# Seven block products in place of eight in 15 of the feed-forward pairs of a two-layer diffusion trunk

## The chip, the cores and the metric

The kernel runs on one core of a Trainium2 chip. The metric is the device time of one execution in microseconds (us). Engines are named as the profile names them: PE is TensorE's matrix multiplies, PEld its weight loads, DVE is VectorE, ACT is ScalarE, POOL is GpSimd, SP is SyncE, which issues the large loads.

## What is computed

Two layers over 256 latent tokens (stream 0) and 256 context tokens (stream 1), model width 1024. Each layer is a gated feed-forward sub-layer (FFN), a mixer of attention and retention, and a second FFN. The last FFN runs for the latent tokens alone. So three FFNs (layer 0 first and second, layer 1 first) have both streams, and one has a single stream.

```
def swiglu_sublayer(h, shift, scale, gate, g_pre, g_post, wi, wo):
    u = rmsnorm(h, g_pre) * (1 + scale) + shift
    a, b = jnp.split(u @ wi, 2, axis=-1)
    y = (jax.nn.silu(a) * b) @ wo
    return h + FFN_RESIDUAL * gate * rmsnorm(y, g_post)
```

The hidden width of an FFN is 22 x 128. `shift`, `scale` and `gate` come from `silu(c) @ ada_w[l] + ada_b[l]`, nine vectors for each layer, which must be ready when the sub-layer that uses them starts.

## The kernel before

**Precision.** Every float32 operand of a large matrix product is split in two float32r parts, hi (a copy, ACT) and lo = x - hi (a subtraction, DVE). A product is then three matmuls: hi hi, hi lo, lo hi.

**An FFN.** The normalized input u lies transposed in SBUF as two tiles, `uh` and `ul`, each 128 partitions x 2 streams x 8 k-tiles x 256 tokens. In the up stage a loop over f = 2 to 21 calls `pair(f)` (line 729; pairs 0 and 1 go through `first` or `first_of_all`). A pair loads two weight tiles of 128 x 1024 (512 KB each; line 160), splits each (`load_w`: hi on ACT, line 167, lo on DVE, line 168), and multiplies: for each of the two tiles and each of the 8 k-tiles `uT` (line 200) issues three matmuls over all 512 tokens, 48 matmuls for the pair. Then `gated` (line 479) forms silu(a) * b on ACT (line 480) and DVE (line 481) into a tile `g`, which is kept until the down stage. In the last FFN only 256 tokens are there, and the same 48 matmuls have 256 columns. There `uu` lies 48 elements further on in its tiles (`SHIFT`, lines 93 and 486).

The down stage (line 866 on) computes y in two halves of 512 columns. Each half takes 11 chunks of two f: `prep` loads and splits one 128 x 1024 tile of `wo` and splits two `g` tiles (lines 879 and 880), and four token tiles take six matmuls each (lines 889 to 891). The last three chunks of a half are done token tile by token tile.

**Work that fills DVE.** The products of `ada_w` with the conditioning are done on DVE in steps (`ada_steps`, line 314): a step loads 512 KB and runs two SCALAR_TENSOR_TENSOR of 128 x 1024 (line 324), one for each stream. `ada.step(n)` puts n steps into the program at a place. `fill` gives their number for the up and the down stage of an FFN: (34, 14) for the first FFN of layer 0, (32, 8) for the second, (30, 10) for the first of layer 1. In the up stage they are spread over the pairs (line 864), in the down stage over the first 12 of 16 chunks: the first eight of half 0 and the first four of half 1 (line 905).

**Order and buffers.** The program is written once, in order; a scheduler at compile time gives each engine its own fixed order, an earlier place in the program first among what it takes to be ready, so work can move ahead of its place where its buffers are free. Buffers are rings: 7 raw tiles for all large loads, 3 `whi` and 3 `wlo`, 2 each of `t4k0` and `t4k1`, 26 tiles of 2 KB (`t2k`: the 22 `g` tiles and short-lived ones), 8 banks of PSUM, and a tile `gm` that serves gates, attention outputs and raw weights in turn.

Of the kernel before, what the change touches and what calls it, by code (L numbers as in the profile page):

```python
# [8 lines left out]
F32 = mybir.dt.float32  # L9
R = mybir.dt.float32r  # L10
# [3 lines left out]
AX = mybir.AxisListType  # L14

P = 128
L = 2
D = 1024
KT = 8
# [13 lines left out]
def hybrid_kernel(ctx: ExitStack, tc: tile.TileContext, A: dict, out: bass.AP):  # L33
# [123 lines left out]
    def load_raw(src, shape):  # L157
        raw = wp.tile([P, 1024], F32, tag="raw", name="raw", bufs=7)
        n = shape[0] * shape[1]
        loads.append(nc.sync.dma_start(raw[:, :n], src).ins)  # L160
        return raw[:, :n].rearrange("p (a b) -> p a b", a=shape[0])

    def load_w(src, shape):
        raw = load_raw(src, shape)
# [240 lines left out]
    def pre_norm(sub, s):  # L405
# [3 lines left out]
            last = pre_norm_part(sub, s, xn, k2)  # L409
        return last  # L410

    def pre_norm_part(sub, s, xn, k2):
        pt = psum([P, 2, 256], "ps_tr")
        for k in (0, 1):
            q, c0 = divmod(128 * (k2 + k), 512)
            for i in (0, 1):
                last = nc.tensor.transpose(pt[:, k, 128 * i:128 * i + 128], xn[i][q][:, c0:c0 + 128], ident)
        uf = t2k([P, 2, 256], name="uf")
        for k in (0, 1):
            sc, sh = scT[:, sub, s, k2 + k:k2 + k + 1], shT[:, sub, s, k2 + k:k2 + k + 1]  # L420
            nc.scalar.activation(uf[:, k, :], pt[:, k, :], AF.Identity, scale=sc, bias=sh)
        hi = uu[0][:, s, k2:k2 + 2, :]
        nc.vector.tensor_copy(hi, uf)
        behind[0] = nc.vector.tensor_sub(uu[1][:, s, k2:k2 + 2, :], uf, hi.bitcast(F32)).ins
        return last.ins

    def post_half(y, gates, t, half, part):


        junk = small([P, 512], "junk", 1)  # L430
        ss = small([P, 1], "ssy", 12)
        nc.scalar.activation(junk, y, AF.Square, scale=D ** -0.5, accum_out=ss)
        if half:
            st = small([P, 1], "ssum", 12)
            nc.vector.scalar_tensor_tensor(out=st, in0=part[0][0], scalar=RMS_EPS, in1=ss, op0=ALU.add, op1=ALU.add)
            ss = rsqrt(st)
        x = t2k([P, 512], name="x")
        nc.vector.tensor_mul(x, y, gates[t // 2][:, 512 * half:512 * half + 512])
        part[half] = ss, x
# [43 lines left out]
    def last_head(then, l, mm, ys, gates, parts):  # L483
# [28 lines left out]
        ssy = {}  # L512

        def square(t, half):
            junk = small([P, 512], "junk", 1)
            ssy[t, half] = small([P, 1], "ssy", 12)
            nc.scalar.activation(junk, ys[half, t], AF.Square, scale=D ** -0.5, accum_out=ssy[t, half])

# [185 lines left out]
    def ffn(l, name, sub, streams, fill, nxt):  # L704
# [6 lines left out]
        def first():  # L711
# [14 lines left out]
                    gated(gf[f][:, cs], *ps)  # L726
            g.extend(gf)

        def pair(f):
            w = [next_w.pop()] if next_w else [load(f, 0)]  # L730
            w.append(load(f, 1))
            ps = [psum([P, n], "ps_up") for _ in range(2)]
            for ab in range(2):
                for k in range(KT):
                    uT(ps[ab], w[ab], k, 0, streams)
            g.append(t2k([P, n], name="g"))
            gated(g[f], *ps)

        def first_of_all():
# [17 lines left out]
            def modulated(j):  # L757


                ks, pt = slice(2 * j, 2 * j + 2), pts.pop(j)  # L760
                uf = [t2k([P, 2, 256], name="uf") for _ in range(2)]
                for outs in [(uh[:, 0, ks, :], uh[:, 1, ks, :]), (uf[1], uf[0])]:
                    if outs[0] is uf[1]:
                        yield
                    for k in (0, 1):
                        kk = 2 * j + k
                        sc, sh = ([x[:, 0, s, kk:kk + 1] for s in range(2)] for x in (scT, shT))
                        a, v = (0, 1) if outs[0] is not uf[1] else (1, 0)
                        nc.scalar.activation(outs[0][:, k, :], pt[a][:, k, :], AF.Identity, scale=sc[a], bias=sh[a])
                        nc.vector.tensor_scalar(out=outs[1][:, k, :], in0=pt[v][:, k, :], scalar1=sc[v],  # L770
                                                scalar2=sh[v], op0=ALU.mult, op1=ALU.add)
                yield
                for s in range(2):
                    behind[0] = nc.vector.tensor_sub(ul[:, s, ks, :], uf[s], uh[:, s, ks, :].bitcast(F32)).ins

            def mm_hi(j, *ws):
# [79 lines left out]
        for f in range(2, NFF):  # L856
# [3 lines left out]
                with tc.issue_after(behind[0]):  # L860
                    constants(loads[-1])
            f0 = 4 if l == 0 and sub == 0 else 2
            if f >= f0:
                ada.step(fill[0] * (f - f0 + 1) // (NFF - f0) - fill[0] * (f - f0) // (NFF - f0))
            pair(f)
        gates = gate_tiles(l, sub, streams)
        parts = [[None, None] for _ in range(nt)]
        for half in range(2):
# [43 lines left out]
    def mixer(l, last):  # L912
# [271 lines left out]
        def ret_out(hd):  # L1184
            for s in range(streams):
# [4 lines left out]
                        nc.tensor.matmul(py[:, i], lhsT=pp[:, 128 * i:128 * i + 128], rhs=vr[kt][:, hd],  # L1190
                                         start=(n_ == 0), stop=(n_ == len(both) - 1))
                y = yrs[:, (streams * hd + s) % 4]
                y2 = small([P, 2, P], "yr2", 1)
                nc.scalar.activation(y2, py[:, :, 1, :], AF.Copy)
                nc.vector.tensor_add(y, py[:, :, 0, :], y2)
                st = small([P, 2, 6], "bst", 4)
# [104 lines left out]
    ada.add(0, (2, 4, 3, 5, 7, 6))  # L1301
    for l in range(L):
        last = l == L - 1
        ffn(l, "ffn1", 0, 2, (34, 14) if l == 0 else (30, 10), 1)
        ada.drain()
        mixer(l, last)

        if not last:
            ada.add(0, (8,))
            ada.add(1, (1, 0, 2, 4, 3, 5, 7, 6, 8))  # L1310
        ffn(l, "ffn2", 2, 1 if last else 2, (0, 0) if last else (32, 8), "out" if last else 0)


# [72 lines left out]
```

## Time and profile before

| | |
|---|---|
| Median of 3 runs | 1682.74 us |
| Lowest and highest | 1679.69 and 1683.19 us |
| The profiled execution: its own time | 1685.35 us |
| Its span, first to last instruction | 1683.6 us |
| Mean granted TensorE clock | 0.999 of full speed |
| PE, PEld, DVE, ACT busy | 99%, 83%, 70%, 45% |
| Read from HBM | 251.74 MB |

The 1.75 us between the span and the own time lie outside the instructions. A busy PE in this table is a sum of overlapping matmuls, each longer than the distance to the next; the pace is read from start to start.

### The profile page before, as it was taken

The numbers are of one execution on the slowest core, as the hardware profiler recorded it, in microseconds if no ns is written. First come the engines' busy times: TensorE is split into PE (matmuls) and PEld (weight loads), VectorE is DVE, ScalarE is ACT, GpSimd is POOL, SyncE is SP. The second block draws the span as 40 slices with busy tenths as digits, with TensorE's granted clock in tenths as the row PEclk, the third lists the DMA queues.
The fourth block names the chain that finished last, engine by engine and source line by source line (L and its number), as shares of the span: only waits on it lengthen the run. The fifth ranks groups of instructions, "written<-read, shape, count | busy, mean of one in ns | idle before, by whom it ended". The sixth has DMA issues, their size and how long they took to land.

```text
span 1683.6 us, 22853 instructions
## 1 busy us (share of the span) xinstructions
PE 1659.0 (99%) x8664; PEld 1400.9 (83%) x8664; DVE 1177.9 (70%) x2119; ACT 749.7 (45%) x1311; POOL 47.9 (3%) x75
## 2 busy tenths in 40 slices
PE   9999999999999999999999999999999999999998
PEld 7888887888778798888888898888888888879986
DVE  5597767757998868666567487665666689865566
ACT  4422223446787652222235452222235578774454
POOL 1000000001000210000000000000000100000000
PEclk9999999999999999999999999999999999999999
DMA  9477555532113216565444346555444222345552
GB/s 366 155 237 244 177 186 191 160 124 82 51 43 109 91 63 224 188 192 170 151 138 151 100 138 206 169 170 168 152 138 148 76 94 80 114 150 186 186 190 86
DMA packets 74479, 254.34 MB, mean 151 GB/s; under 512 B 8576, under 2 KB 13168, under 8 KB 74240
## 3 DMA queue, kind: packets, MB, share of 16 engines
q1 hardware_dynamic: 73632, 251.15, 45.7%
q0 software_dynamic: 736, 1.72, 0.3%
q8 instruction: 68, 1.11, 0.3%
q14 instruction: 43, 0.35, 0.1%
HBM read 251.74 MB, written 1.10 MB: 150 GB/s over the span
## 4 chain that ended last, share of the span: by engine, by line
PE 83%; DVE 7%; ACT 4%; DMA 2%; issue 2%; POOL 1%; SPq 0%; DVEq 0%; POOLq 0%; ACTq 0%
PE ps_up L206 16%; PE ps_up L205 16%; PE ps_up L207 16%; PE ps_dn L889 7%; PE ps_dn L890 7%; PE ps_dn L891 7%; DMA raw<-in_ada_w 2%; PE ps_pk L215 1%; PE ps_pk L217 1%; PE ps_pk L216 1%; PE ps_po L1047 1%; PE ps_pj L205 1%; PE ps_pj L206 1%; PE ps_pj L207 1%; DVE wlo L168 1%
## 5 line engine op out<-in xcount | busy, mean ns | idle before, releaser
L167 ACT ACTIVATE whi<-raw 128x1024 fp32r<-128x1024 f32 x291 | 308.2, 1060 | 761.3 <-PE ps_up L206 496.4
L168 DVE TENSOR_TENSOR wlo<-raw,whi 128x1024 fp32r<-128x1024 f32 x291 | 355.2, 1222 | 188.5 <-ACT whi L167 185.8
L205 PE MATMUL ps_up<-uh,whi 128*128 128x512 f32 (+1 forms) x1352 | 483.6, 358 | 0.0
L207 PE MATMUL ps_up<-uh,wlo 128*128 128x512 f32 (+1 forms) x1352 | 483.0, 357 | 0.0
L206 PE MATMUL ps_up<-ul,whi 128*128 128x512 f32 (+1 forms) x1352 | 483.0, 357 | 0.0
L324 DVE SCALAR_TENSOR_TENSOR yr<-raw,cbc 128x1024 f32<-128x1024 f32 x256 | 313.0, 1223 | 164.8 <-DMA raw<-in_ada_w 161.4
L205 PEld LDWEIGHTS ps_up<-uh,whi 128*128 128x128 f32 x1352 | 255.5, 189 | 37.6
L207 PEld LDWEIGHTS ps_up<-uh,wlo 128*128 128x128 f32 x1352 | 254.1, 188 | 37.1
L206 PEld LDWEIGHTS ps_up<-ul,whi 128*128 128x128 f32 x1352 | 254.1, 188 | 37.0
L890 PE MATMUL ps_dn<-whi,ghl 128*128 128x512 f32 x560 | 218.0, 390 | 2.1 <-DVE ghl L880 2.1
L891 PE MATMUL ps_dn<-wlo,ghl 128*128 128x512 f32 x560 | 217.9, 389 | 0.0
L889 PE MATMUL ps_dn<-whi,ghl 128*128 128x512 f32 x560 | 217.0, 391 | 0.8 <-ACT ghl L879 0.6
L890 PEld LDWEIGHTS ps_dn<-whi,ghl 128*128 128x128 f32 x560 | 105.1, 188 | 25.0 <-DVE ghl L880 3.1
L889 PEld LDWEIGHTS ps_dn<-whi,ghl 128*128 128x128 f32 x560 | 104.6, 188 | 24.9 <-ACT ghl L879 3.6
L891 PEld LDWEIGHTS ps_dn<-wlo,ghl 128*128 128x128 f32 x560 | 105.1, 188 | 21.8
L880 DVE TENSOR_TENSOR ghl<-g,ghl 128x512 fp32r<-128x512 f32 (+1 forms) x176 | 102.3, 618 | 0.4
L879 ACT ACTIVATE ghl<-g 128x512 fp32r<-128x512 f32 (+1 forms) x176 | 91.9, 564 | 14.9 <-DVE g L481 7.6
L481 DVE TENSOR_TENSOR g<-g,ps_up 128x512 f32<-128x512 f32 (+1 forms) x90 | 54.2, 602 | 46.1 <-PE ps_up L207 45.1
L205 PE MATMUL ps_pj<-uh,whi 128*128 128x256 f32 (+1 forms) x168 | 58.6, 349 | 0.0
L206 PE MATMUL ps_pj<-ul,whi 128*128 128x256 f32 (+1 forms) x168 | 56.0, 333 | 0.1
L207 PE MATMUL ps_pj<-uh,wlo 128*128 128x256 f32 (+1 forms) x168 | 55.6, 331 | 0.0
L480 ACT ACTIVATE g<-ps_up 128x512 f32<-128x512 f32 (+1 forms) x90 | 46.3, 514 | 2.6 <-PE ps_up L207 2.6
(282 smaller groups left out, 2013.0 us busy)
## 6 DMA issues: line engine op xcount, KB each, us to landing
raw<-in_ffn_wi SPq DMA_DIRECT2D x172, 512.0 KB, 4.1
raw<-in_ada_w SPq DMA_DIRECT2D x138, 512.0 KB, 4.2
raw<-in_ffn_wo SPq DMA_DIRECT2D x88, 512.0 KB, 3.4
raw<-in_w_in SPq DMA_DIRECT2D x20, 512.0 KB, 3.3
raw<-in_w_in_t SPq DMA_DIRECT2D x16, 512.0 KB, 3.3
raw<-in_w_out SPq DMA_DIRECT2D x16, 512.0 KB, 3.6
gate<-gd SPq DMA_DIRECT2D x10, 512.0 KB, 4.9
rawg<-in_ada_w SPq DMA_DIRECT2D x4, 512.0 KB, 7.6
```

Of the source, the lines that this page charges most:

```text
L167: nc.scalar.activation(hi, raw, AF.Copy)
L168: nc.vector.tensor_sub(lo, raw, hi.bitcast(F32))
L205: nc.tensor.matmul(ps, lhsT=hi, rhs=mhi, start=(k == 0), stop=False)
L206: nc.tensor.matmul(ps, lhsT=hi, rhs=mlo, start=False, stop=False)
L207: nc.tensor.matmul(ps, lhsT=lo, rhs=mhi, start=False, stop=(k == KT - 1))
L324: nc.vector.scalar_tensor_tensor(out=junk, in0=wr, scalar=1.0, in1=cbc[:, st, :], op0=ALU.mult, op1=ALU.mult, accum_out=v[:, st, k:k + 1])
L481: nc.vector.tensor_mul(gs, gs, b)
L879: nc.scalar.activation(g2[0][i], g[2 * c + i], AF.Copy)
L880: nc.vector.tensor_sub(g2[1][i], g[2 * c + i], g2[0][i].bitcast(F32))
L889: nc.tensor.matmul(y, lhsT=ghi[i][:, cs], rhs=hi[i], start=(f == 0), stop=False)
L890: nc.tensor.matmul(y, lhsT=glo[i][:, cs], rhs=hi[i], start=False, stop=False)
L891: last = nc.tensor.matmul(y, lhsT=ghi[i][:, cs], rhs=lo[i], start=False, stop=(f == NFF - 1))
```

## The change

In the three FFNs with both streams the pairs f = 5, 7, 9, 11 and 13 are computed by `combined(f)`. The product of a pair is a 2 x 2 block matrix (gate and value weights by the two halves of the 1024 inputs) times a 2 x 2 block matrix (the two halves of the inputs by the two streams). Seven block products replace the eight: each has 4 k-tiles x 3 matmuls of 256 columns, 84 matmuls for a pair. Sums of weight blocks are formed on DVE in the raw tiles, in place; the raw tile of the first weights is split twice, before and after. Four mixed blocks of u are made once per FFN by `combine_u`, after pair 2, and are held in both `t4k` rings, four `t2k` tiles and `gm` until pair 13 is done. The float32 copies of u (`uf`) are kept for it.

The `ada` steps move: none at the five pairs, and `fill` becomes (26, 22), (24, 16) and (24, 16) in the order of the FFNs given above. Two scratch tiles change (`junk` to bfloat16, `yr2` into `t2k`). The ring slots of `whi` and `wlo` grow by 128 elements, because a combined pair puts its weights 80 elements into a slot (`BACK`).

```
+COMBINED = (5, 7, 9, 11, 13)
+    BACK = 80
...
+        if sub != 1:
+            ufs[s, k2] = uf
...
+        def combine_u():
+            t1, t2_ = ([t4k(i, [P, 4, 256], R, name="tu") for i in (0, 1)] for _ in range(2))
+            t3 = [[t2k([P, 2, 256], R, name="tu") for _ in range(2)] for _ in range(2)]
+            gm = act.tile([P, 2, 4, 256], R, tag="gm", name="tug")
+            for q in range(2):
+                b11, b12, b21, b22 = (ufs.pop((s, 4 * r + 2 * q)) for r in range(2) for s in range(2))
+                ks = slice(2 * q, 2 * q + 2)
+                nc.vector.tensor_sub(b22, b12, b22)
+                nc.vector.tensor_sub(b12, b11, b12)
+                nc.vector.tensor_sub(b11, b22, b11)
+                nc.vector.tensor_add(b21, b11, b21)
+                for x, hi, lo in ((b12, t1[0][:, ks], t1[1][:, ks]), (b11, t2_[0][:, ks], t2_[1][:, ks]),
+                                  (b22, t3[0][q], t3[1][q]), (b21, gm[:, 0, ks], gm[:, 1, ks])):
+                    nc.scalar.activation(hi, x, AF.Copy)
+                    nc.vector.tensor_sub(lo, x, hi.bitcast(F32))
...
+        def combined(f):
+            r1, r2 = (load_raw(wi[l, 2 * f + ab], (KT, P)) for ab in range(2))
+            a11, a12, a21, a22 = r1[:, :4], r1[:, 4:], r2[:, :4], r2[:, 4:]
+            def buffer():
+                both = [wp.tile([P, KT * P + 128], R, tag=n_, name=n_, bufs=3) for n_ in ("whi", "wlo")]
+                return [x[:, BACK:BACK + KT * P].rearrange("p (k c) -> p k c", c=P) for x in both]
+            def split(x, hl, n0=0):
+                n1 = n0 + x.shape[1]
+                nc.scalar.activation(hl[0][:, n0:n1], x, AF.Copy)
+                nc.vector.tensor_sub(hl[1][:, n0:n1], x, hl[0][:, n0:n1].bitcast(F32))
+            def product(w, n0, u):
+                ps = psum([P, LAT], "ps_up")
+                for k in range(4):
+                    for n_, (i, j) in enumerate(((0, 0), (0, 1), (1, 0))):
+                        nc.tensor.matmul(ps, lhsT=w[i][:, n0 + k, :], rhs=u(j, k), start=(k == 0 and n_ == 0),
+                                         stop=(k == 3 and n_ == 2))
+                return ps
...
+            wa = buffer()
+            split(r1, wa)
+            wd = [t2k([P, 4, P], R, name="wd") for _ in range(2)]
+            split(a22, wd)
+            nc.vector.tensor_add(a22, a21, a22)
+            nc.vector.tensor_add(a21, a11, a21)
+            wc = buffer()
+            split(r2, wc)
+            nc.vector.tensor_add(a11, a11, a22)
+            nc.vector.tensor_add(a12, a12, a11)
+            wb = buffer()
+            split(r1, wb)
+            nc.scalar.activation(p1, product(wa, 0, mix["b", 0, 0]), AF.Copy)
+            nc.vector.tensor_add(lat, product(wa, 4, mix["b", 1, 0]), p1)
+            nc.scalar.activation(lat, lat, AF.Silu)
+            nc.scalar.activation(p7, product(wc, 0, mix[3]), AF.Copy)
+            nc.vector.tensor_add(e, product(wd, 0, mix[4]), p7)
+            p5 = product(wc, 4, mix[1])
+            nc.vector.tensor_add(u2, product(wb, 0, mix[2]), p1)
+            nc.vector.tensor_sub(e, e, u2)
+            nc.vector.tensor_mul(lat, lat, e)
+            nc.vector.tensor_add(u2, p5, u2)
+            nc.vector.tensor_sub(e, p7, u2)
+            nc.vector.tensor_add(cx, product(wb, 4, mix["b", 1, 1]), u2)
+            nc.scalar.activation(cx, cx, AF.Silu)
+            nc.vector.tensor_mul(cx, cx, e)
+            g.append(gt)
...
-            if f >= f0:
-                ada.step(fill[0] * (f - f0 + 1) // (NFF - f0) - fill[0] * (f - f0) // (NFF - f0))
-            pair(f)
+            if f >= f0 and not (streams == 2 and f in COMBINED):
+                some = [x for x in range(f0, NFF) if streams == 1 or x not in COMBINED]
+                i = some.index(f)
+                ada.step(fill[0] * (i + 1) // len(some) - fill[0] * i // len(some))
+            if streams == 2 and f in COMBINED:
+                combined(f)
+            else:
+                pair(f)
+            if streams == 2 and f == 2:
+                combine_u()
+        mix.clear()
...
-                y2 = small([P, 2, P], "yr2", 1)
+                y2 = t2k([P, 2, P], name="yr2")
...
-        ffn(l, "ffn1", 0, 2, (34, 14) if l == 0 else (30, 10), 1)
+        ffn(l, "ffn1", 0, 2, (26, 22) if l == 0 else (24, 16), 1)
...
-        ffn(l, "ffn2", 2, 1 if last else 2, (0, 0) if last else (32, 8), "out" if last else 0)
+        ffn(l, "ffn2", 2, 1 if last else 2, (0, 0) if last else (24, 16), "out" if last else 0)
```

## Rows read from the trace of the kernel before

**Rows 1.** The page, parts 1 and 2: engines over the span, PE by slices.

```profile
PE 1659.0 (99%) x8664; PEld 1400.9 (83%) x8664; DVE 1177.9 (70%) x2119; ACT 749.7 (45%) x1311; POOL 47.9 (3%) x75
...
PE   9999999999999999999999999999999999999998
```

**Rows 2.** Busy time by stretch: length, PE, PEld, DVE, ACT, POOL, clock, DMA.

```profile
52.00:74.00 22.00, 22.00 (x99) 18.22 (x98) 9.04 (x10) 7.30 (x11) 0.00 (x0) 1.00 0.42 143
...
160.00:282.00 122.00, 121.78 (x538) 100.44 (x536) 84.11 (x131) 30.91 (x37) 0.50 (x1) 1.00 0.56 184
282.00:326.00 44.00, 42.51 (x186) 34.90 (x187) 36.39 (x55) 14.72 (x22) 0.00 (x0) 1.00 0.54 173
...
342.00:364.00 22.00, 22.00 (x99) 18.23 (x98) 12.10 (x16) 8.98 (x14) 0.00 (x0) 1.00 0.40 125
...
896.00:940.00 44.00, 43.95 (x193) 35.85 (x192) 27.92 (x41) 22.35 (x37) 0.00 (x0) 1.00 0.43 141
...
1263.00:1307.00 44.00, 43.42 (x191) 35.69 (x192) 28.09 (x41) 22.29 (x36) 0.00 (x0) 1.00 0.42 140
...
1506.00:1616.00 110.00, 110.00 (x936) 110.00 (x935) 57.47 (x64) 47.73 (x64) 0.00 (x0) 1.00 0.59 191
```

**Rows 3.** Timeline of PE, first FFN, 512 columns: first and last of 24 starts.

```profile
99.76 0.39 PE L206 MATMUL ps_up<-ul,whi 128*128 128x512 f32 x1
...
104.97 0.39 PE L205 MATMUL ps_up<-uh,whi 128*128 128x512 f32 x1
```

**Rows 4.** Timeline of PE, last FFN, 256 columns: first and last of 53 starts.

```profile
1539.77 0.28 PE L207 MATMUL ps_up<-uh,wlo 128*128 128x256 f32 x1
...
1545.89 0.28 PE L205 MATMUL ps_up<-uh,whi 128*128 128x256 f32 x1
```

**Rows 5.** Timeline of PE, pair 0 of layer 1, 256 columns: first and last of 23 starts.

```profile
985.25 0.28 PE L206 MATMUL ps_up<-ul,whi 128*128 128x256 f32 x1
...
987.88 0.28 PE L207 MATMUL ps_up<-uh,wlo 128*128 128x256 f32 x1
```

**Rows 6.** Timeline of DVE where it runs without a gap, layer 0, second FFN.

```profile
623.93 0.41 DVE L481 TENSOR_TENSOR g<-g,ps_up 128x256 f32<-128x256 f32 x1
624.26 0.69 DVE L424 TENSOR_TENSOR ul<-uf,uh 128x512 fp32r<-128x512 f32 x1
624.87 1.22 DVE L324 SCALAR_TENSOR_TENSOR yr<-raw,cbc 128x1024 f32<-128x1024 f32 x1
...
626.13 1.23 DVE L324 SCALAR_TENSOR_TENSOR yr<-raw,cbc 128x1024 f32<-128x1024 f32 x1
...
630.15 1.22 DVE L168 TENSOR_TENSOR wlo<-raw,whi 128x1024 fp32r<-128x1024 f32 x1
631.28 1.22 DVE L324 SCALAR_TENSOR_TENSOR yr<-raw,cbc 128x1024 f32<-128x1024 f32 x1
```

**Rows 7.** Groups of ACT instructions by line and shape: busy, mean ns, idle before.

```profile
L167 ACT ACTIVATE whi<-raw 128x1024 fp32r<-128x1024 f32 x291 | 308.2, 1060 | 761.3 <-PE ps_up L206 496.4 <-PE ps_dn L890 187.7 <-issue 31.8
...
L480 ACT ACTIVATE g<-ps_up 128x256 f32<-128x256 f32 x28 | 10.4, 371 | 0.0
```

**Rows 8.** Waits of DVE, 160 to 282 us: total, times, longest.

```profile
DVE yr L324 <- DMA raw<-in_ada_w: 40.4, 14, 5.5
```

**Rows 9.** Waits of DVE, 282 to 364 us: total, times, longest.

```profile
DVE wlo L168 <- ACT whi L167: 17.2, 9, 3.5
DVE yr L324 <- DMA raw<-in_ada_w: 4.3, 3, 2.2
```

**Rows 10.** The one wait of PE, 250 to 320 us: total, times, longest.

```profile
PE ps_dn L890 <- DVE ghl L880: 1.7, 1, 1.7
```

More of the change, by code (lines that the diff above doesn't have):

```diff
@@ L410, in pre_norm @@
         return last
+    ufs = {}
     def pre_norm_part(sub, s, xn, k2):
@@ L424, in pre_norm_part @@
         behind[0] = nc.vector.tensor_sub(uu[1][:, s, k2:k2 + 2, :], uf, hi.bitcast(F32)).ins
+        if sub != 1:
+            ufs[s, k2] = uf
         return last.ins
     def post_half(y, gates, t, half, part):
-        junk = small([P, 512], "junk", 1)
+        junk = t2.tile([P, 512], B16, tag="junk", name="junk", bufs=1)
         ss = small([P, 1], "ssy", 12)
@@ L514, in square @@
         def square(t, half):
-            junk = small([P, 512], "junk", 1)
+            junk = t2.tile([P, 512], B16, tag="junk", name="junk", bufs=1)
             ssy[t, half] = small([P, 1], "ssy", 12)
@@ L727, in first @@
             g.extend(gf)
+        mix = {}
+        def combine_u():
[13 more added lines that the diff above has]
+                    nc.vector.tensor_sub(lo, x, hi.bitcast(F32))
+            mix[1] = lambda i, k: t1[i][:, k, :]
+            mix[2] = lambda i, k: t2_[i][:, k, :]
+            mix[3] = lambda i, k: t3[i][k // 2][:, k % 2, :]
+            mix[4] = lambda i, k: gm[:, i, k, :]
+            for n_, (r, st) in enumerate(((0, 0), (1, 0), (1, 1))):
+                mix["b", r, st] = lambda i, k, r=r, st=st: (uh, ul)[i][:, st, 4 * r + k, :]
@@ new lines, in combined @@
+        def combined(f):
[15 more added lines that the diff above has]
+                return ps
+            gt = t2k([P, n], name="g")
+            lat, cx = gt[:, :LAT], gt[:, LAT:]
+            sa, sd = (t2k([P, 2, LAT], name="sv") for _ in range(2))
+            p1, p7, u2, e = sa[:, 0], sa[:, 1], sd[:, 0], sd[:, 1]
+            wa = buffer()
[25 more added lines that the diff above has]
+            g.append(gt)
@@ L773, in modulated @@
                 for s in range(2):
+                    ufs[s, 2 * j] = uf[s]
                     behind[0] = nc.vector.tensor_sub(ul[:, s, ks, :], uf[s], uh[:, s, ks, :].bitcast(F32)).ins
```

## The prediction

> **What bounds the kernel now.** I read the page first. PE is busy 99% of the span and no slice but the last shows less than nine tenths [rows 1]. That alone proves little, because matmuls overlap, so I next read the distance from one matmul start to the next. In an up stage with both streams 24 starts span 5.21 us: 0.2265 us for 512 columns [rows 3]. A whole pair of 48 matmuls is then 10.87 us. The stretch from 160 to 282 us holds 538 matmuls, and 122 / 538 is 0.2268 us: the pace of the sample is the pace of the stage, with no gap worth the name [rows 2]. The one wait of PE around the step from up to down stage is 1.7 us [rows 10]. So in the FFNs PE's column stream sets the time and everything else hides under it, at a granted clock of 1.00, its upper level of 2.4 GHz [rows 2]. A change to an FFN pays exactly what it takes from PE, until DVE, the next engine, becomes late.
>
> DVE was read by stretch. Before the first down stage it works 84 of 122 us [rows 2], and of the rest 40.4 us (some of it before the stretch) are waits for `ada_w` loads [rows 8], that is for filler work, which nothing on PE needs soon. Right behind the step into the down stage DVE works 36.4 of 44 us [rows 2].
>
> **PE's part.** Each combined pair drops 48 matmuls of 512 columns and adds 7 x 4 x 3 = 84 of 256. The trace has 256-column matmuls from the same helper in two places: 0.1177 us from start to start in the last FFN (6.12 us / 52) [rows 4] and 0.1195 us in pair 0 of layer 1 (2.63 us / 22) [rows 5]. They bound the combined pair at 9.89 and 10.04 us, a gain of 0.98 or 0.83 us over 10.87. The two places differ in the code by where u lies: 48 elements further on in the last FFN. The new weights lie 80 elements into their slots, with u at 0, and -48 and 80 are the same place modulo 128. If that distance is what matters, which is an estimate from the code, the three products that multiply unmixed u run at 0.1177. The other four read mixed blocks from other tiles; for them I take the middle, 0.1186. That gives 0.1182 on average, 9.93 us a pair, 0.94 us gained. Fifteen pairs: **-14.1 us**, ends -12.5 and -14.7.
>
> **The stream of short matmuls, weighed.** Half the columns cost 52% of the time [rows 3, 4], so PE pays nearly nothing for the matmul count. The Trainium skill, page "TensorE: Matmul & The Clock Gate", section "Back-to-back issue gap", has another price: a sustained stream at about 131 ns for 512 columns and 81 ns for 128. By those figures 84 matmuls of even 128 columns take 6.8 us against 6.3 us for 48 long ones, and the change would lose 0.5 us a pair, +7.5 us in place of -14.1 (an estimate from that page). The trace disagrees by 1.7 times at 512 columns, and the measurement decides.
>
> **What DVE gets.** Where it runs without a gap a 1024-column lo takes 1.13 us (630.15 to 631.28), a 512-column operation 0.61, a 256-column operation 0.33, an `ada` step 2 x 1.26 = 2.5 us [rows 6]. A plain pair costs 2 x 1.13 + 0.61 = 2.9 us and its filler 26/13 = 2 steps or fewer, 5.0 us. A combined pair costs three lo of 1024, one lo and four sums of 512, nine operations of 256: 3.4 + 3.05 + 3.0 = 9.4 us, without filler. Two neighbours, combined and plain, are 17.3 us of DVE under 9.93 + 10.87 = 20.8 us of PE: 83%. DVE keeps up on average. ACT has 3 x 1.06 + 0.6 + 4 x 0.37 = 5.3 us in the combined pair and is no limit [rows 7]. In detail the third `whi`/`wlo` slot comes free when PE leaves the plain pair, and it is needed five products later, 5 x 12 x 0.1182 = 7.1 us; ACT and DVE need 2.2 us for it. The next plain pair's first weights get their slot 2.8 us into the combined pair and have 7.1 us. These covers are thinner than before, where a slot was free a whole tile (5.4 us) ahead of a 2.2 us need and DVE had 30% of its time free. If a pair of `ada` operations stands ahead of such a split and an eviction behind it, up to a microsecond can show. I take **+0.5 us for each of the three FFNs, +1.5 us**; nothing and +1 us a combined pair are the ends that matter (the latter is a rival).
>
> **Making the mixed blocks.** `combine_u` is sixteen DVE operations of 512 columns, 9.8 us, and eight ACT copies, about 5 us. In the first FFN DVE works 9 of the 22 us after pair 2 starts [rows 2], so it fits. In the other two it pushes aside `ada` steps that run ahead of their place, which only shortens their lead. I take nothing; without that cover it would be late for pair 5 by what is left of 9.8 us after three plain pairs of slack, 3 x (10.87 - 7.9) = 8.9 us, so at most 1 us. Holding `t4k` until pair 13 takes away early splits of `g` for the down stage, which have eight pairs to catch up. Loads from HBM are the same in number and only keep two of seven raw tiles longer.
>
> **Moved filler.** The down stages get 22, 16 and 16 steps in place of 14, 8 and 10. Spread over 12 of the chunks, the first eight chunks of half 0 get 14 (from 9), 10 (from 5) and 10 (from 6); the first four of half 1 get 8 (from 5), 6 (from 3) and 6 (from 4). In the first FFN that is 5 x 2.5 = 12.5 us more in a stretch where DVE is idle 7.6 us of 44 [rows 2]: 4.9 us short, unless steps run ahead in the last eight pairs of the up stage, where DVE has 8 x (10.87 - 7.9) = 24 us free and raw tiles limit it. Half 1 needs 7.5 us more against 9.9 idle from 342 to 364 us. In the second FFN 12.5 us go into 16.1 idle, in the third 10 us into 15.9 [rows 2]: they fit. Idle time there is partly waits of the lo for its hi (17.2 us), which is waiting for PE to free a slot and can be filled [rows 9]. I take **+1.5 us** in the first FFN; ends 0 and +12.5. `prep` of the next chunk stands behind the steps on DVE, and PE waits for it.
>
> `junk`, `yr2` and the larger slots I cost at nothing: the same instructions on the same engines, and none of the rows shows a wait for them.
>
> **Sum.** -14.1 + 1.5 + 1.5 = -11.1 us. The profiled execution has 1683.6 us of span and 1685.35 of its own; it becomes 1674.3. The median of the runs lies 2.6 us under that, so from 1682.74 the forecast is 1671.6, rounded to 1672.
>
> **Rivals.**
> - *The down stage of the first FFN is bound by DVE.* The steps do not run ahead, since DVE there already waits for their loads [rows 8], and the late `prep` stalls PE for the whole 12.5 us. With the other terms: 1682.7 - 14.1 + 1.5 + 12.5 = 1682.6, no change; half of it is 1676. For it: 7.6 us idle against 12.5 [rows 2]. Against: the 24 us free before.
> - *DVE is late in the combined pairs: slower.* One `ada` step of the neighbour (2.5 us) stands in each of the fifteen ahead of the lo that PE needs next. From 0.94 us lost a pair on the change stops paying; at 2.5 us it is 15 x (2.5 - 0.94) = +23 us, 1706. For it: 83% use on a strictly ordered queue, and a chain of sum, hi, lo, sum, hi, lo in each pair. Against: `ada` may run ahead of its place, and the present stage at 70% loses nothing.
> - *Short matmuls cost more than their rows.* If the mixed operands, read from five different tiles, cost more than 10.87 / 84 = 0.1294 us a matmul, the gain is gone: 1685 with the stalls. For it: only that no row has these operand pairs. Against: every 256-column row is at 0.118 to 0.120 [rows 4, 5]. The Trainium skill's figures under "Back-to-back issue gap" ("TensorE: Matmul & The Clock Gate") would land here, at 1690 before stalls by the estimate above; [rows 3] speak against them.
>
> **How the numbers follow.** A gain or loss under 0.2%, 3.4 us, is no change here. The forecast has 0.72, and its own ends are 1667 (no stall, best pace, and a microsecond of chance in the mixers) and 1678. The first rival has 0.13, nearly all of it no change; the second 0.10, slower; the third 0.05, split between no change and slower. So faster 0.73, no change 0.15, slower 0.12. The range reaches from 1666 to 1683, the whole of the first rival, and leaves out the second and most of the third.
>
> **What would show it.** In the changed profile 84 matmuls of 256 columns start 0.1177 to 0.1195 us apart in each of fifteen pairs of about 9.9 us, with no idle PE inside them, and the clock stays at 1.00. DVE's busy time rises by 15 x (9.4 - 2.9) + 3 x 9.8 = 127 us, from 1178 to about 1305 us (a little more in sums of durations, which overlap), ACT's by some 55. In the first down stage PE shows one or two waits for `ghl` or `wlo`, 1 to 3 us. A pair of 10.9 us or more, PE waiting for `wlo` or `wd` inside combined pairs, or a down stage of the first FFN more than 4 us longer than now would make the prediction wrong.

## The result and the profile after

The changed kernel takes **1693.28 us** (median of 6 runs, 1687.21 to 1694.56) where the kernel before takes 1682.97 us beside it (6 runs): ratio **1.0057**, interval 1.0036 to 1.0078. Forecast was a gain of 11 us; it lost 10. The profiled execution has 1693.31 us of its own and a span of 1691.5 us.

The page after, part 1, answers to [rows 1]:

```profile
PE 1654.3 (98%) x9204; PEld 1418.4 (84%) x9204; DVE 1304.3 (77%) x2377; ACT 799.3 (47%) x1410; POOL 48.4 (3%) x75
```

DVE's 1304.3 us are the forecast 1305 and ACT's +50 us near the forecast +55: the instructions are the ones that were counted. PE's busy time fell by 4.7 us only. To find where, the span is cut into its stages, each from the first matmul of a stage to the first of the next. Of after, the windows of the first up stage, the first mixer, the two other up stages with both streams and the second mixer; columns as in [rows 2]:

```profile
18.70:273.00 254.30, 248.90 (x1370) 210.14 (x1371) 206.78 (x372) 88.44 (x129) 4.39 (x2) 0.99 0.60 201
...
397.40:617.10 219.70, 213.07 (x1184) 176.15 (x1183) 182.13 (x471) 152.90 (x338) 14.29 (x19) 0.99 0.23 74
617.10:856.70 239.60, 238.09 (x1350) 209.68 (x1349) 192.42 (x308) 86.36 (x130) 2.19 (x4) 1.00 0.49 160
...
979.60:1217.90 238.30, 238.23 (x1350) 209.49 (x1349) 193.24 (x309) 86.39 (x129) 2.19 (x4) 1.00 0.51 163
...
1340.60:1493.00 152.40, 144.00 (x857) 120.82 (x855) 130.50 (x308) 111.76 (x232) 9.21 (x13) 0.99 0.29 92
```

The same cut for every kernel of this study that the argument needs (us; FFN 1 to 3 are those with both streams, the last FFN has 131 or 127 us of up stage and 61 of down stage; "before" and "after" are the two kernels, the other rows the experiments, whose numbers stand in brackets):

| kernel | up 1 | down 1 | mixer 1 | up 2 | down 2 | up 3 | down 3 | mixer 2 |
|---|---|---|---|---|---|---|---|---|
| before | 252.0 | 123.9 | 214.2 | 242.6 | 122.1 | 242.5 | 122.6 | 146.4 |
| after | 254.2 | 124.4 | 219.7 | 239.6 | 122.9 | 238.3 | 122.7 | 152.4 |
| `yr2` alone (2) | 252.0 | 123.6 | 218.2 | 242.5 | 122.1 | 242.5 | 122.0 | 152.6 |
| ring of 27 (3) | 252.0 | 122.2 | 220.1 | 242.5 | 122.1 | 242.5 | 121.9 | 152.6 |
| ring of 29 (4) | 253.9 | 124.6 | 218.2 | 245.3 | 122.5 | 242.5 | 121.9 | 152.6 |
| six raw tiles (5) | 252.3 | 125.1 | 213.9 | 248.4 | 122.3 | 242.5 | 122.0 | 146.4 |
| in turn (6) | 252.0 | 122.4 | 222.0 | 242.6 | 122.1 | 242.5 | 122.0 | 156.6 |
| `yr2` out of the ring (1) | 254.1 | 123.7 | 214.2 | 239.2 | 122.2 | 238.6 | 122.5 | 146.4 |
| two FFNs (7) | 252.0 | 122.0 | 214.1 | 238.4 | 122.4 | 238.5 | 122.0 | 146.4 |
| sums first (8) | 248.6 | 122.8 | 214.1 | 237.9 | 122.2 | 238.3 | 122.1 | 146.5 |
| ada from 6 (9) | 248.6 | 127.1 | 214.2 | 237.8 | 122.5 | 238.3 | 122.1 | 146.5 |
| six pairs (10) | 247.6 | 126.9 | 214.1 | 236.9 | 122.2 | 237.3 | 122.0 | 146.4 |

The last up stage comes at about 131 or 127 us whatever was edited, and the times of the kernel before lie in two groups some 4 us apart, so that stage is not read as an effect, and medians of runs and sums of stages may differ by such an amount.

After against before: the mixers, where no product changed, +5.5 and +6.0 us; the three up stages +2.2, -3.0 and -4.2, together -5.0; the down stages +1.4 in all. Sum +7.9 us, the difference of the two spans (1691.5 - 1683.6).

**Inside the up stages** the combined pair is as forecast. PE's timeline of after, the start and the end of one combined pair and the first long matmul of the next (the transpose at 726.09 is filler):

```profile
716.17 0.28 PE L780 MATMUL ps_up<-uh,whi 128*128 128x256 f32 x1
716.29 0.28 PE L780 MATMUL ps_up<-ul,whi 128*128 128x256 f32 x1
...
725.98 0.28 PE L780 MATMUL ps_up<-uh,wlo 128*128 128x256 f32 x1
726.09 0.27 PE L243 MATMUL ps_mt<-ident,adav 128*16 128x128 f32 x1
726.12 0.48 PE L208 MATMUL ps_up<-uh,whi 128*128 128x512 f32 x1
```

From first to last of 84 starts it is 9.80 us, 0.1181 us each. A pair takes 9.92 us to the next pair's first matmul (forecast 9.93), this one with its transpose 9.95. Twelve of the fifteen take that. The other three take 13.97 (f = 5, first FFN; of it some 0.45 are two long matmuls of the next pair that run inside it), 13.50 (f = 13, first FFN) and 11.71 us (f = 13, second FFN): 9.0 us lost. With 15 x (10.87 - 9.92) = 14.2 us gained, -5.2 us are left, and the stages show -5.0.

The 0.1181 is a mean of two paces. In this pair the six products whose weights lie in the `whi` and `wlo` slots, 80 elements in, run at 0.1178 us a matmul from start to start, those with mixed u no slower than those with unmixed u; the product of `wd` and `gm`, whose weights lie at the start of a `t2k` tile, runs at 0.1200.

PE's waits in the first up stage and the down stage behind it (total, times, longest):

```profile
PE ps_up L780 <- ACT whi L773: 3.1, 2, 2.9
PE ps_up L780 <- DVE wlo L774: 1.5, 1, 1.5
...
PE ps_dn L986 <- ACT ghl L976: 2.2, 1, 2.2
```

The wait of 1.5 us is at f = 13, and right behind it stands a stretch at half clock (0.50, the level of 1.2 GHz); two more are in the mixers, and one more stretch lies at the very end, as it does before:

```profile
178.50:181.90 3.40, 3.40 (x18) 3.40 (x17) 3.40 (x6) 0.78 (x2) 0.00 (x0) 0.50 0.86 276
...
571.00:574.40 3.40, 3.40 (x9) 2.63 (x8) 1.96 (x4) 1.34 (x3) 0.00 (x0) 0.50 0.00 0
1468.80:1472.20 3.40, 3.21 (x9) 2.55 (x10) 1.46 (x3) 2.69 (x7) 0.00 (x0) 0.51 0.52 154
```

Each costs up to 1.7 us, if PE has work throughout (an estimate: 3.4 us at half pace). The kernel before has none ahead of its end.

**Inside the mixers** the order of ACT's work is another. ACT's timeline of before and then of after, where the first head's retention output begins (`yr`: L1194 is L1291 after, its scaling L1209 is L1306; `dt` and `wt` are the decay tables of a later head):

```profile
546.61 0.39 ACT L1194 ACTIVATE yr<-ps_ry 128x256 f32<-128x256 f32 x1 [2.46 <-PE ps_ry L1190]
546.89 0.52 ACT L1147 ACTIVATE dt<-a 128x384 f32<-128x384 f32 x1
547.54 0.38 ACT L1194 ACTIVATE yr<-ps_ry 128x256 f32<-128x256 f32 x1
547.82 0.59 ACT L1153 ACTIVATE wt<-edge,lgk,lg 128x256 f32<-128x256 f32 x1
...
549.66 0.70 ACT L1209 ACTIVATE yr<-yr,rgn 128x128 f32<-128x128 f32 x2 [0.26 <-POOL rgn L1203]
```

```profile
550.30 0.38 ACT L1291 ACTIVATE yr<-ps_ry 128x256 f32<-128x256 f32 x1 [3.29 <-PE ps_ry L1287]
551.08 0.39 ACT L1291 ACTIVATE yr<-ps_ry 128x256 f32<-128x256 f32 x1 [0.40 <-PE ps_ry L1287]
553.77 0.69 ACT L1306 ACTIVATE yr<-yr,rgn 128x128 f32<-128x128 f32 x2 [2.30 <-POOL rgn L1300]
555.42 0.69 ACT L1306 ACTIVATE yr<-yr,rgn 128x128 f32<-128x128 f32 x2 [0.95 <-POOL rgn L1300]
556.02 0.51 ACT L1244 ACTIVATE dt<-a 128x384 f32<-128x384 f32 x1
```

Before, `dt` comes 0.3 us after the first `yr`, and the tables fill the time in which POOL computes the scale. After, `dt` comes 5.7 us after it, behind the whole output of the earlier head; ACT idles 2.30 and 0.95 us on POOL instead. PE meets it at the output transposes. These are its waits there in the second mixer, 1.4 us before and 4.1 after (in the first 1.0 and 3.1):

```profile
PE ps_ro L1215 <- ACT yr L1209: 1.4, 2, 1.1
```

```profile
PE ps_ro L1312 <- ACT yr L1306: 4.1, 3, 2.7
```

The one edit that touches this part is `yr2`, the scratch of these `yr` copies, moved from a slot of its own into the ring `t2k`.

### The profile page after: what moved, and what is told of

Read it like the earlier page. It is cut to its first block, busy times and chain, and to the rows that moved or that the text cites. A ratio compares the mean times of both kernels' runs of the same rounds, so it can differ in the third digit from the quotient of the medians.

```text
span 1691.5 us, 24295 instructions
## 1 busy us (share of the span) xinstructions
PE 1654.3 (98%) x9204; PEld 1418.4 (84%) x9204; DVE 1304.3 (77%) x2377; ACT 799.3 (47%) x1410; POOL 48.4 (3%) x75
## 4 chain that ended last, share of the span: by engine, by line
PE 80%; DVE 9%; ACT 4%; issue 3%; DMA 2%; POOL 1%; DVEq 0%; POOLq 0%; ACTq 0%; SPq 0%
PE ps_up L208 12%; PE ps_up L210 12%; PE ps_up L209 12%; PE ps_dn L987 7%; PE ps_dn L988 7%; PE ps_dn L986 7%; PE ps_up L780 7%; DMA raw<-in_ada_w 2%; DVE yr L327 1%; DVE wlo L171 1%; PE ps_pk L218 1%; PE ps_pk L220 1%; PE ps_po L1144 1%; PE ps_pk L219 1%; PE ps_pj L208 1%
## 5 line engine op out<-in xcount | busy, mean ns | idle before, releaser
L170 ACT ACTIVATE whi<-raw 128x1024 fp32r<-128x1024 f32 x261 | 276.0, 1059 | 517.8 <-PE ps_up L209 255.3
L171 DVE TENSOR_TENSOR wlo<-raw,whi 128x1024 fp32r<-128x1024 f32 x261 | 318.8, 1223 | 156.1 <-ACT whi L170 155.4
L208 PE MATMUL ps_up<-uh,whi 128*128 128x512 f32 (+1 forms) x1112 | 390.5, 351 | 0.3 <-ACT whi L170 0.2
L209 PE MATMUL ps_up<-ul,whi 128*128 128x512 f32 (+1 forms) x1112 | 389.8, 351 | 0.0
L210 PE MATMUL ps_up<-uh,wlo 128*128 128x512 f32 (+1 forms) x1112 | 389.5, 350 | 0.0
L327 DVE SCALAR_TENSOR_TENSOR yr<-raw,cbc 128x1024 f32<-128x1024 f32 x256 | 313.0, 1223 | 83.1 <-DMA raw<-in_ada_w 80.6
L210 PEld LDWEIGHTS ps_up<-uh,wlo 128*128 128x128 f32 x1112 | 210.4, 189 | 27.8
L208 PEld LDWEIGHTS ps_up<-uh,whi 128*128 128x128 f32 x1112 | 209.1, 188 | 28.3 <-ACT whi L170 0.9
L209 PEld LDWEIGHTS ps_up<-ul,whi 128*128 128x128 f32 x1112 | 209.1, 188 | 27.3
L987 PE MATMUL ps_dn<-whi,ghl 128*128 128x512 f32 x560 | 218.2, 390 | 1.1 <-DVE ghl L977 1.1
L773 ACT ACTIVATE whi<-raw 128x1024 fp32r<-128x1024 f32 x45 | 47.8, 1063 | 88.9 <-DVE raw L794 40.1
L780 PE MATMUL ps_up<-tu,whi 128*128 128x256 f32 x360 | 65.6, 282 | 3.1 <-ACT whi L773 3.1
L780 PEld LDWEIGHTS ps_up<-tu,whi 128*128 128x128 f32 x360 | 55.6, 191 | 3.5 <-ACT whi L773 3.5
```

What stands on the lines that cost most here:

```text
L170: nc.scalar.activation(hi, raw, AF.Copy)
L171: nc.vector.tensor_sub(lo, raw, hi.bitcast(F32))
L208: nc.tensor.matmul(ps, lhsT=hi, rhs=mhi, start=(k == 0), stop=False)
L209: nc.tensor.matmul(ps, lhsT=hi, rhs=mlo, start=False, stop=False)
L210: nc.tensor.matmul(ps, lhsT=lo, rhs=mhi, start=False, stop=(k == KT - 1))
L327: nc.vector.scalar_tensor_tensor(out=junk, in0=wr, scalar=1.0, in1=cbc[:, st, :], op0=ALU.mult, op1=ALU.mult, accum_out=v[:, st, k:k + 1])
```

## The experiments

**1 and 2: `yr2` out of the ring, and `yr2` alone.** The first is the changed kernel with `yr2` in a fixed place again, the one slot of `junk`:

```
-                y2 = t2k([P, 2, P], name="yr2")
+                y2 = t2.tile([P, 2, P], F32, tag="junk", name="yr2", bufs=1)
```

> The changed kernel, but yr2 has one fixed slot of its own again (it shares the 1 KB slot of junk) and no longer takes one of the 26 t2k tiles. Theory A (yr2 in the t2k ring pushes back the next retention head's decay tables and scores): both mixers return to the times of before, 214 and 146 us in place of 220 and 152, the two drops of the clock in them go, and the run is 11 us faster than the changed kernel, about 1682 us. Theory B (the mixers lose because all other tiles of SBUF moved, or because of the FFN's steps): the mixers stay at 220 and 152 us and the time at 1693.

Measured: 1680.14 us (12 runs), ratio 0.9998, interval 0.9987 to 1.0009. The second is the kernel before with the change's line:

```
-                y2 = small([P, 2, P], "yr2", 1)
+                y2 = t2k([P, 2, P], name="yr2")
```

> The kernel before with one line of the change: yr2 goes into the t2k ring. Everything else, the FFNs too, is as before. Theory A (the ring is full there): mixers of about 220 and 152 us, +11 us, 1694 us. Theory B (placement of tiles or the FFNs): mixers as before, 1683 us.

Measured: 1692.11 us (6 runs), ratio **1.0076**, interval 1.0058 to 1.0095. The mixers are 214.2 and 146.4 us in the first, 218.2 and 152.6 in the second (table). This one line costs as much as the whole change lost, within the intervals. Without it the seven products stand even with the kernel before by the medians; in the profiles, both with the long last up stage, the three up stages are 5.2 us and the span 6.1 us shorter, so the medians may hide some gain.

The order can be read in full from the traces. In both mixers ACT's instructions stand in one and the same order in the kernel before and in experiment 1, and in one other order in the kernel after and in experiment 2; DVE's do likewise. Between the two orders some 60 of ACT's 337 instructions and some 110 of DVE's 470 in the first mixer have changed their place. The order explains the 218.2 us of experiment 2; the kernel after has the same order and 219.7, and it alone of the two has a stretch at half clock in that mixer.

**3: a ring with one tile more** (the kernel of experiment 2 with 27 tiles in `t2k`; `junk` in bfloat16 makes the room; the fence shows the ring's line alone).

```
-        return t2.tile(shape, dt, tag="t2k", name=name, bufs=26)
+        return t2.tile(shape, dt, tag="t2k", name=name, bufs=27)
```

> As e2_yr2_alone (the kernel before with yr2 in the t2k ring), and the ring has 27 tiles in place of 26; junk is bfloat16 to make the room. Theory A (the ring is one tile short while retention heads overlap, and the next head's tables wait for a tile): most of the loss of e2_yr2_alone goes, about 1680 to 1683 us, mixers near 214 and 146 us. Theory C (one more tile does not help, because what counts is that yr2 asks for tiles in turn with the tables, or several tiles are missing): 1690 us or more, mixers near 218 and 152 us.

Measured: 1692.44 us, ratio 1.0064 (1.0044 to 1.0084), mixers 220.1 (with a stretch at half clock) and 152.6 us. One tile more does not bring the mixers back.

**4 and 5: three tiles more, and its twin.** The kernel of experiment 2 with 29 tiles, paid for with `junk` in bfloat16 and one of seven slots of `raw`; the twin, the kernel before with six slots of `raw`, pays without getting anything (not shown: the lines of `yr2` and `junk`, and the change of 7 to 6 in two more places).

```
-        return t2.tile(shape, dt, tag="t2k", name=name, bufs=26)
+        return t2.tile(shape, dt, tag="t2k", name=name, bufs=29)
...
-        raw = wp.tile([P, 1024], F32, tag="raw", name="raw", bufs=7)
+        raw = wp.tile([P, 1024], F32, tag="raw", name="raw", bufs=6)
```

> The kernel before with `yr2` taking its two tiles from the 2 KB ring, as the change does, and with that ring at 29 tiles instead of 26; the room comes from `junk` held as bf16 and from the ring `raw` of the weight loads, which has 6 slots instead of 7. If the mixers' 4 to 6 us come from too few tiles (two heads need about 27, and two more with `yr2` on top), 29 are enough: the mixers take 214.2 and 146.4 us as before, or what the twin of this run with 6 slots of `raw` takes. If they come from the order in which the ring hands tiles out, so that `yr2` and the next head's tables stand in one line however long the ring is, the mixers stay 4 to 6 us longer than the twin's, about 218 to 220 and 152.6 us, and the whole run about 9 us longer than the twin.

> The twin: the kernel before with 6 slots instead of 7 in the ring `raw` of the weight loads and nothing else. It prices what the run with 29 tiles gives up for its room. Expected by both theories: mixers at 214.2 and 146.4 us, whole time within 0.5% of the kernel before, or some us longer where the weights' loads arrive late in the up stages.

Measured: 1696.26 us, ratio 1.0092 (1.0074 to 1.0110), against the twin's 1691.18 us, 1.0065 (1.0043 to 1.0087). The mixers are 218.2 and 152.6 us with 29 tiles, 213.9 and 146.4 us in the twin. So up to three tiles more don't help the mixers. The whole run is 5 us over its twin where 9 were expected: the mixers lose 10.5 us, and the second up stage is 3.1 us shorter than the twin's, which was not followed up. The twin cost more than the 0.5% expected: with one raw slot fewer the second up stage takes 248.4 us, from 242.6.

**6: the order alone.** The kernel before, `yr2` in its own slot; only ACT's issue order is fixed to that of the program. `issue_after` orders instructions of one engine and waits for nothing. The lines shown are those added or changed, the rest is left out.

```
+            with behind_turn(turn[0]):
+                dt, wt = decay(hd)
...
+                    turn[0] = nc.scalar.activation(hi, pm, AF.Copy).ins
...
+            scored = turn[0]
...
+                with behind_turn(scored):
+                    nc.scalar.activation(y2, py[:, :, 1, :], AF.Copy)
...
+                    turn[0] = nc.scalar.activation(y[:, i], y[:, i], AF.Copy, scale=r[:, i:i + 1]).ins
```

> The kernel before, `yr2` in its own slot as there; only the order of ACT in the retention part is fixed to program order: the tables of a later head behind the scaling of the earlier head's output, and the copies `yr` of a head behind the last `pmh` of the scores written before it. No tile moves. If the 4 to 6 us of each mixer come from this order, which the shared ring forces because it hands out tiles in the order of the program, the mixers take 218 to 220 and about 152.6 us and the whole run is 0.5 to 0.8% longer than the kernel before. If they come from the tiles themselves (their place in SBUF, or tiles that are missing), the mixers stay at 214.2 and 146.4 us and the ratio at 1.000.

Measured: 1697.15 us, ratio **1.0105** (1.0075 to 1.0134), mixers 222.0 and 156.6 us. ACT's timeline of this kernel at the same place as above:

```profile
545.27 0.39 ACT L1203 ACTIVATE yr<-ps_ry 128x256 f32<-128x256 f32 x1 [2.46 <-PE ps_ry L1198]
546.21 0.39 ACT L1203 ACTIVATE yr<-ps_ry 128x256 f32<-128x256 f32 x1 [0.55 <-DVE yr L1204]
548.33 0.70 ACT L1218 ACTIVATE yr<-yr,rgn 128x128 f32<-128x128 f32 x2 [1.73 <-POOL rgn L1212]
549.50 0.70 ACT L1218 ACTIVATE yr<-yr,rgn 128x128 f32<-128x128 f32 x2 [0.48 <-POOL rgn L1212]
550.11 0.51 ACT L1153 ACTIVATE dt<-a 128x384 f32<-128x384 f32 x1
```

At this place it is the order of after, and the mixers lose 7.8 and 10.2 us, with no tile moved (stretches at half clock, 6.8 us in the first and 3.4 in the second, are by estimate 3.4 and 1.7 us of it). It is not the order of after everywhere: some 24 of ACT's 337 instructions in the first mixer stand elsewhere, and the loss is larger. So it is shown that an order of this kind costs such a time by itself, and that the one line of `yr2` changes the order and costs the time. That the ring brings it about by handing out tiles in the order of the program, so that the next head's tables, written later, ask behind `yr2`, fits experiments 3 to 5 and was not seen directly.

**7: two FFNs.** Experiment 1 with the first FFN as before the change, ten combined pairs left and its `fill` at (34, 14) again (one line of the edit is shown).

```
+        mixed = COMBINED if streams == 2 and (l, sub) != (0, 0) else ()
...
```

> As e1_yr2_own, and the first FFN of layer 0 is left without combined pairs, with its old steps (34, 14). Ten combined pairs are left. Theory A (in the first FFN the combined pairs lose about 7 us of waits and half clock for 4.7 us of gain, the other two FFNs gain 3 and 4.3 us): 2 to 3 us faster than e1_yr2_own, about 1679 us, first up stage as before. Theory B (every combined pair gains, the waits would be there without them): 4.7 us slower than e1_yr2_own, about 1687 us.

Measured: 1675.32 us, ratio 0.9968 (0.9955 to 0.9980). That is 4.8 us under experiment 1, where 2 to 3 were expected. Scheduled as in experiment 1, seven products pay in the second and third FFN and lose in the first.

**8: the weight sums first.** Experiment 1 with one line of `combined` changed: the `ada` steps written after a combined pair are issued on DVE behind its last weight sum.

```
-            nc.vector.tensor_add(a12, a12, a11)
+            behind[0] = nc.vector.tensor_add(a12, a12, a11).ins
```

> As e1_yr2_own, and in the program of DVE the ada steps of later pairs may not stand ahead of the last weight sum of a combined pair (each later step is ordered behind it). Theory A (what delays the second weights of pair 13 in each FFN, and in part of pair 5 in the first, is ada steps that the scheduler put between the sums): the pairs of 11.7, 11.3 and 10.3 us become 9.9, the 15.5 us of the first pair 5 shrink by 2 to 5 with the drop of the clock behind it, 5 to 8 us less than e1_yr2_own, 1673 to 1675 us. Theory B (the loads come late because two raw tiles are held longer): those pairs keep their length and the time stays at 1680.

Measured: **1667.47 us**, ratio **0.9920** (0.9904 to 0.9935), 12.7 us under the kernel before and 12.7 under experiment 1, where 5 to 8 were expected. Of the 11.8 us between the profiled spans of experiments 1 and 8, 7.1 lie in the three up stages; 4.2 lie in the last up stage (131 and 127 us), which no edit touched. What moved is seen on DVE at the first combined pair. After (L327 is an `ada` operation, L793 and L794 the first two sums, L774 the lo of the summed weights; PE's longest wait there, 2.9 us, is for the hi, which waits for the same sums):

```profile
85.64 1.22 DVE L327 SCALAR_TENSOR_TENSOR yr<-raw,cbc 128x1024 f32<-128x1024 f32 x1
...
86.87 0.69 DVE L793 TENSOR_TENSOR raw<-raw 128x512 f32<-128x512 f32 x1
...
87.55 1.23 DVE L327 SCALAR_TENSOR_TENSOR yr<-raw,cbc 128x1024 f32<-128x1024 f32 x1
...
89.45 0.69 DVE L794 TENSOR_TENSOR raw<-raw 128x512 f32<-128x512 f32 x1
...
90.14 1.23 DVE L327 SCALAR_TENSOR_TENSOR yr<-raw,cbc 128x1024 f32<-128x1024 f32 x1
...
91.36 1.23 DVE L774 TENSOR_TENSOR wlo<-raw,whi 128x1024 fp32r<-128x1024 f32 x1
```

With the sums first:

```profile
85.95 0.69 DVE L793 TENSOR_TENSOR raw<-raw 128x512 f32<-128x512 f32 x1
...
86.68 0.69 DVE L794 TENSOR_TENSOR raw<-raw 128x512 f32<-128x512 f32 x1
...
88.81 1.22 DVE L774 TENSOR_TENSOR wlo<-raw,whi 128x1024 fp32r<-128x1024 f32 x1
```

From the first sum to the lo it is 2.86 us instead of 4.49 (4.49 in experiment 1 too), although two more sums now stand between them. Fourteen of the fifteen pairs take 9.92 us, the first 11.34. In the first up stage PE is left with one wait inside the pairs, and the stage runs at full clock:

```profile
PE ps_up L780 <- DVE wlo L774: 1.0, 1, 1.0
```

```profile
18.90:267.50 248.60, 247.03 (x1369) 208.72 (x1370) 209.81 (x375) 89.24 (x129) 4.39 (x2) 1.00 0.62 206
```

**9: `ada` two pairs later in the first FFN** (experiment 8 with `f0 = 6`), meant to mend pair 5.

```
-            f0 = 4 if l == 0 and sub == 0 else 2
+            f0 = 6 if l == 0 and sub == 0 else 2
```

> As e4_sums_first, and in the first FFN the ada steps begin at pair 6 in place of pair 4, so none stands on DVE ahead of the sums of pair 5. Theory A (steps of pair 4 and the chain of small constants operations hold the sums of pair 5): pair 5 of the first FFN at 10 to 11 us, 1 to 3 us less than e4_sums_first unless later waits take them. Theory B (the wait for GpSimd in the constants alone holds it): same as e4_sums_first within 1 us.

Measured: 1673.92 us, ratio 0.9957 (0.9941 to 0.9972): worse than experiment 8 by 6.5 us. Pair 5 still takes 11.40 us, and the down stage behind it grows to 127.1 us. In that down stage DVE is full (9.96 of 10 us), PE waits 2.7 us for a `ghl` where experiment 8 waits 0.4, and the clock falls to 0.50 behind the wait. The `ghl` is ACT's copy, and ACT had itself waited 4.2 us for a `ghl` operation of DVE:

```profile
310.00:320.00 10.00, 7.28 (x28) 5.13 (x27) 9.96 (x16) 2.73 (x4) 0.00 (x0) 0.94 0.63 205
318.80:322.20 3.40, 3.40 (x10) 2.63 (x9) 3.37 (x6) 0.00 (x0) 0.00 (x0) 0.50 0.79 258
```

```profile
ACT ghl L976 <- DVE ghl L977: 4.2, 1, 4.2
...
PE ps_dn L986 <- ACT ghl L976: 2.7, 1, 2.7
```

This is the first rival of the prediction, at about a third of its 12.5 us, in a kernel that gives DVE one plain pair less for its filler (12 instead of 13).

Neither theory gives the time. Pair 5 by itself did as the second one had it: with no `ada` step ahead of its sums it is as long as in experiment 8. What still stands ahead of them on DVE is the chain of small constants, with a wait of 2.8 us for POOL in it, here and in experiment 8 alike:

```profile
DVE wz L137 <- POOL z L135: 2.8, 1, 2.8
```

**10: a sixth pair** (experiment 8, `COMBINED` with 15).

```
-COMBINED = (5, 7, 9, 11, 13)
+COMBINED = (5, 7, 9, 11, 13, 15)
```

> As e4_sums_first with a sixth combined pair, 15, in each of the three FFNs. If DVE still has room, three more pairs gain 0.95 us each, 2.9 us in all. If DVE or the t2k tiles are now short (16 g tiles and the mixed blocks are held at once), pairs 13 and 15 show waits and it is no faster or slower than e4_sums_first.

Measured: 1671.53 us, ratio 0.9941 (0.9926 to 0.9956). Each up stage is 1.0 us shorter, as a pair should give, and beyond the first of all no combined pair takes more than 9.95 us, pairs 13 and 15 neither. But the first down stage is 4.1 us longer (126.9), with a wait of 2.4 us for `ghl` and half clock behind it. With the steps spread as they are, five pairs are what DVE's slack in the first FFN carries; that DVE is short there is read from the same wait as in experiment 9.

**11: the weights at the start of their slots** (the changed kernel).

```
-    BACK = 80
+    BACK = 0
```

> The changed kernel with the weights of a combined pair at the start of their slots (BACK = 0). If the distance between weights and u modulo 128 elements sets the pace, the products of unmixed u go from 0.1177 to 0.120 us a matmul and those of t4k blocks may too: up to 72 x 0.0023 = 0.17 us a pair, 2.5 us in all. If the place does not matter: 0.118 as in the changed kernel, and no difference.

Measured: 1695.69 us, one run. An undisturbed pair here, its first matmul and the first of the next pair:

```profile
1060.41 0.28 PE L780 MATMUL ps_up<-uh,whi 128*128 128x256 f32 x1
...
1070.48 0.40 PE L208 MATMUL ps_up<-uh,whi 128*128 128x512 f32 x1
```

10.07 us against 9.92: 0.15 us a pair, 2.2 us for fifteen, 0.1199 us a matmul against 0.1181. The place of the weights, 80 elements into their slots, matters, as the prediction had estimated from [rows 4, 5], and without it the pace is just past the dearer of the two ends taken there (0.1195). All products but the one with `wd`, whose place did not change, become slower; it keeps its 0.1200. That it is the distance to u modulo 128 elements, and not the place of the weights alone, was not tested.

## Why the prediction was wrong

- **The step that failed is "`junk`, `yr2` and the larger slots I cost at nothing".** The reason given, the same instructions on the same engines, is true and not enough: the engines' order is fixed by a scheduler that looks at when buffers come free, and the new place of `yr2` put the next head's tables behind the earlier head's output on ACT (shown by experiments 1 and 2, and for the order by itself by experiment 6). Measured +5.5 and +6.0 us in the mixers, and 1.0076 for the line alone. "None of the rows shows a wait for them" spoke of rows of waits that all lie outside the mixer, and of the order of before, which is what changed. For `junk` and the larger slots nothing was right: experiment 1 keeps both, and its mixers take what they took before.
- **The PE term was right, its split in part by luck.** -14.1 us was forecast from 0.1177 us for three products and 0.1186 for the four with mixed u; 0.1181 was measured, 9.92 us a pair against 9.93. But it was six products at 0.1178 and one at 0.1200: three of the four products with mixed u are as fast as the others, and the one slower product is the one whose weights have no `BACK`. The Trainium skill's rule ("TensorE: Matmul & The Clock Gate", section "Back-to-back issue gap"), by which, in the prediction's estimate, the change would have lost 7.5 us here, fails on its figure for 512 columns, 131 ns, where [rows 3] have 226.5 ns; the 0.1181 us measured for 256 columns lie between its figures for 128 and 512.
- **The stalls "+0.5 us for each of the three FFNs" were too small in the first.** Each up stage should fall by five pairs, 4.7 us; the stages came out 6.9, 1.7 and 0.5 us above that. The mechanism is the one named as the second rival, `ada` operations ahead of what PE needs next, but in three pairs of fifteen, and ahead of the weight sums more than of the lo. Experiment 8 orders the sums ahead and brings them to 1.3, 0 and 0.5 us above it: 1.8 us for the three where 1.5 was forecast.
- **The clock "stays at 1.00"** failed too: by estimate up to 1.7 us in the first up stage (inside the +6.9) and in each mixer.
- **`combine_u`, at nothing or at most 1 us:** right. The last operation of `combine_u` on DVE ends at 62.1 us after, 23 us ahead of the first combined pair, and 22 us ahead of it in each of the other two FFNs. The 3.6 us that this pair loses after, and the 1.42 with the sums first, are not its cost; ahead of the sums stand `ada` steps and the constants with their 2.8 us for POOL, which the prediction does not name. What of the 1.42 each of these makes was not tried alone.
- **The first down stage, +1.5 us:** it took +0.5, with one wait of 2.2 us for `ghl` that was forecast as 1 to 3 us. The first rival did not happen in this kernel; experiments 9 and 10 show it, at about a third of its price, one step away.
- The third rival, dearer short matmuls, is excluded by 0.1181 us against its limit of 0.1294.

With both faults mended (experiment 8) the kernel gains 12.7 us, where 11.1 had been forecast for the change as it stands. Part of the difference is the first down stage, which in the profile takes 1.1 us less than before where 1.5 more were forecast.

## What to carry to other kernels

Where a scheduler fixes the order of the engines, a scratch tile that changes its ring is an edit to that order: look at the timeline of every engine that writes or reads the tile, in its own stage, before costing it at nothing. Fewer matmuls pay while the engine that prepares their operands keeps up; here a few pairs with filler between the steps of that chain ate most of what the others gained, and an ordering edge behind its last step took 7.1 us off the three up stages (experiment 1 against 8) and made no other stage longer. Where PE is the limit and fully fed, a pair's gain could be forecast from its pace to 0.01 us, so the work of a forecast belongs to the waits.

## What the runs showed that was not expected

- After a wait of PE the granted clock sometimes fell to 0.50 for about 3.4 us, so that a wait of 1.5 us cost 3.6 (the pair of 13.50 us) and one of 2.7 us cost over 4 (experiment 9). Not every wait does it: the 2.9 us at f = 5 after left the clock at 1.00, a wait as long at the same place in experiment 1 was followed by 0.50 from 91.1 us on. What decides was not tested.
- The same 256-column matmuls of the last FFN, at 0.1177 us in [rows 4], start 0.1133 us apart in the profile of experiment 8 (first and last of 55 starts), in a stage that no edit touched:

```profile
1526.01 0.28 PE L209 MATMUL ps_up<-ul,whi 128*128 128x256 f32 x1
...
1532.13 0.28 PE L209 MATMUL ps_up<-ul,whi 128*128 128x256 f32 x1
```

Over the stage this is the difference between 131 and 127 us. Its cause stays open.
- Seven slots for raw weights are not spare: with six the second up stage is 5.8 us longer, by estimate 1.7 us of it a stretch at half clock.
